# A decoder block's output projections behind attention: where inputs, results and gates are buffered, and when they are loaded

## The chip, the cores and the metric

The kernel runs on one core of a Trainium2 chip. The metric is the device time of one execution in microseconds; of several runs the median is given. A core has a matrix engine (PE, whose weight loads are a row of their own, PEld), a vector engine (DVE), a scalar engine (ACT), a general engine (POOL) and SyncE (SP), which here only issues transfers. Each engine takes its instructions in program order. "ACTq" and "SPq" mark what an engine's queue issues, transfers among it.

## The reference

One layer of a decoder block for 2048 tokens of width 1024, in float32. It has two branches, a gated linear recurrence and dilated windowed attention, each projected to 1024 columns; the two are merged with sigmoid gates and projected once more.

```
y_rnn  = (hr * silu(z_rnn)) @ w_out_rnn
y_attn = (o  * silu(z_attn)) @ w_out_attn
merged = sigmoid(g_r + bg_r) * y_rnn + sigmoid(g_a + bg_a) * y_attn
x      = x + gate * (merged @ w_o)
out    = rms_norm(x, g_final)
```

## The kernel before

**Precision.** Every float32 operand of a matmul is kept as two parts: a rounded high part, written by ACT (`hi_act`, L158), and the rest, a subtraction on POOL (`lo_pool`, L164) or DVE (`lo_dve`, L167). One product is three matmuls, high by high, high by low and low by high (`mm3`, all issued in L150).

**Work so far.** The input projections and the recurrence come first, then attention. Intermediate results lie in device memory, transposed: `oT` (attention, already times its gate), `yaT` (recurrence), `grT` and `gaT` (the merge gates), `mrT` (the recurrence's gated half of the merge), `meT` (the merged input of the last projection), `gateD` (the residual gate), and the output weights as they are in `wR` or split in `wD`.

**The two branch projections** are `steps` (L1658). There are eight jobs: the recurrence's output weights with four groups of 512 tokens, then attention's with the same four. A job has 8 tiles (one of 128 output columns each), a tile 8 steps over the inner dimension, a step 3 matmuls of 128x512. The 40 tiles t = 0 to 39 are laid between attention's operations. The last 24 (t = 40 to 63, from `TAIL0` = 40; jobs 5, 6 and 7, all of them attention's weights) come behind attention, and with them the loop `for s in range(LAST)` of 192 steps, s = 0 to 191. I count "steps of the tail" by this s. In these tiles a tile needs:

- *weights*, in two halves of four steps (`load_w`, L1675): raw from `wR` by SP into one of six buffers (S0 to S3, st3, st4), five halves ahead; `split_w` (k % 4 == 2) splits them two halves ahead, the low part on DVE for even halves and on POOL for odd ones;
- *inputs* y, eight slices of 128x512 for a job (`load_y`, `split_y`): load and split stand in the tables `LATE_LOAD_Y` and `LATE_SPLIT_Y`, by a step x that is 0 at the first step of the job's predecessor's last tile and 8 at the first step of the job itself. The split parts (`yh`, `yl`) have nine buffers each. The first five raw slices go to the four buffers R0 to R3 (`load_yd`, L346), the last three to the stages st1 and st2 (L1693);
- *gates*, two tiles `fg` from `gaT` and `mrT` out of four buffers (`load_g`, L1712), for tile t + 1 at k = 3 of tile t;
- *the eviction* of the tile before at k = 1 (`evict`): product times gate (L1718), plus the recurrence's half (L1720), both on DVE. The result goes to one of two buffers, s1 and s2 (the last two tiles: into the gate's buffer);
- *the store* of the tile before at k = 6 (`store`, L1726) to `meT`, by SP.

**Built beside the tail:** the right operands of the last projection. It uses a Strassen scheme (seven products instead of eight), so W_o, with its rows scaled by the residual gate, is turned into seven operands B11, T2, T3, T1, B21, T4, B22, each in a high and a low tile (`h`, `l`) of four 128x512 slices. `build_rows(x, k)` makes slice k of all of them from two rows of 128x1024 in st1 and st2: two gatings on POOL (L1859), combinations (L1867) and four low parts on DVE, three low parts on POOL, seven high parts on ACT. It starts at step x = 14, 75, 100 and 142 and is spread over 21 steps. The rows are loaded by `load_rows` (L1856) at x - 7 and x - 4, by SP for k = 0 and by ACT's queue otherwise. I call these builds 0 to 3.

**Behind the tail** comes the output stage, `output_pair`: eight pairs of 128 rows with seven products of 12 matmuls each, then the final norm.

What sets the order: everything here stands in `tc.manual_schedule()`, so that each engine takes its instructions as the code issues them. Waits for buffers follow from who used a buffer last. Transfers of SP and ACT share eight semaphores in turn: a transfer is issued only when the eighth before it has landed.

Of the kernel before, what the change touches and what calls it, by code (L numbers as in the profile page):

```python
# [10 lines left out]
F32 = mybir.dt.float32  # L11
# [9 lines left out]
P = 128  # L21
S = 2048
D = 1024
KT = D // P
NB = 4
CH = 512
H = 8
KH = KT // 2
# [61 lines left out]
def decoder_block(ctx, tc, x, c, positions, g_norm, w_mod, b_mod, w_in, b_gate, conv_w, conv_b,  # L90
# [4 lines left out]
    def T(pool, shape, dt, tag, **kw):  # L95
        cnt[0] += 1
        return pool.tile(shape, dt, tag=tag, name=f"{tag}_{cnt[0]}", **kw)
# [59 lines left out]
    def hi_act(o, i):  # L157
        nc.scalar.activation(o, i, AF.Copy)  # L158
# [175 lines left out]
    n_w, n_y, W, Y0 = [0], [0], {}, {}  # L334
# [151 lines left out]
    B = {}  # L486
# [10 lines left out]
    pR = pools.open("pR", side="right", bufs=1)  # L497
# [611 lines left out]
    for t in range(6):  # L1109
        pieces = []  # L1110
        i0 = t * P
        while i0 < (t + 1) * P:
            hd, i = divmod(i0, 96)
            n = min(96 - i, (t + 1) * P - i0)
# [154 lines left out]
    for f in range(2):  # L1269
# [20 lines left out]
        n = 0  # L1290
# [363 lines left out]
    TAIL0 = KT * (NB + 1)  # L1654
# [3 lines left out]
    def steps(jobs):  # L1658

        tiles = [(j, m) for j in range(len(jobs)) for m in range(KT)]  # L1660
        Y, G = {}, {}

        def load_w(x):

            if x < 2 * len(tiles):
                assert x == n_w[0]
                j, m = tiles[x // 2]
                if x <= RAW:
                    load_wd(jobs[j][0], m, x % 2)
                    return  # L1670

                n_w[0] += 1
                i = (x - 2 * TAIL0) % 6
                W[x] = t = T(pS, [P, 2, KH, P], F32R, f"S{i}") if i < 4 else T(fp, [P, 2, KH, P], F32R, f"st{i - 1}")
                nc.sync.dma_start(t[:, 1].bitcast(F32), wR[m, x % 2])  # L1675

        def split_w(x):
            if RAW < x < 2 * len(tiles):
                raw = W[x][:, 1].bitcast(F32)
                hi_act(W[x][:, 0], raw)  # L1680
                (lo_pool if x % 2 else lo_dve)(W[x][:, 1], raw, W[x][:, 0])

        def load_y(j, k, t):
            if j < len(jobs):
                w, ys, n = jobs[j]
                assert ys is yaT or (n // 2, k, n % 2) in stored
                if t >= TAIL0 and k > 4:
                    n_y[0] += 1
                    i, half = divmod(k - 5, 2)
                    if half == 0:  # L1690
                        v["y", j] = stage(1 + i, [P, D])
                    Y0[False, n, k] = y = v["y", j][:, half * CH : (half + 1) * CH]
                    nc.sync.dma_start(y, ys[k * P : (k + 1) * P, n * CH : (n + 1) * CH])  # L1693
                    return
                load_yd(ys, n, k)

        def split_y(j, k):
            if j < len(jobs):
                Y[j, k] = yh, yl = [T(fl, [P, CH], F32R, tag, bufs=NY) for tag in ("yh", "yl")]
                w, ys, n = jobs[j]  # L1700
                t = Y0.pop((ys is yaT, n, k))
                hi_act(yh[:], t[:])
                (lo_dve if k % 2 else lo_pool)(yl[:], t[:], yh[:])

        def load_g(t):
            j, m = tiles[t]
            w, ys, n = jobs[j]
            at_ = slice(m * P, (m + 1) * P), slice(n * CH, (n + 1) * CH)
            G[t] = []
            for src in (grT,) if ys is yaT else (gaT, mrT):  # L1710
                g = T(fl, [P, CH], F32, "fg", bufs=4)
                nc.sync.dma_start(g[:], src[at_])  # L1712
                G[t].append(g)

        def evict(t, ps):
            g = G[t]
            o = T(fp, [P, CH], F32, f"s{1 + t % 2}") if TAIL0 <= t < TAIL0 + 22 else g[0]
            nc.vector.tensor_tensor(o[:], ps[:], g[0][:], ALU.mult)  # L1718
            if len(g) > 1:
                nc.vector.tensor_tensor(o[:], o[:], g[1][:], ALU.add)  # L1720
            g[0] = o

        def store(t):
            j, m = tiles[t]
            w, ys, n = jobs[j]
            nc.sync.dma_start((mrT if ys is yaT else meT)[m * P : (m + 1) * P, n * CH : (n + 1) * CH], G.pop(t)[0][:])  # L1726

        for k in range(KT):
            split_y(0, k)
        yield  # L1730
        last = None
        for t, (j, m) in enumerate(tiles):
            ps = T(pj, [P, CH], F32, "pj")
            for k in range(KT):
                x = 2 * t + k // KH
                if k % KH == 1:

                    if x < 2 * TAIL0:
                        load_w(x + 3)
                    for x1 in range(x + 3 if x == 2 * TAIL0 else x + 5, x + 6) if x >= 2 * TAIL0 else ():  # L1740
                        load_w(x1)
                if k % KH == 2 and x >= 2 * TAIL0:
                    split_w(x + 2)
                if k == 1 and t:
                    evict(t - 1, last)
                if t < TAIL0:
                    if k == 3:
                        load_g(t)
                    if k == 7 and t:
                        store(t - 1)  # L1750
                else:
                    if k == 0 and t == TAIL0:
                        load_g(t)
                    if k == 3 and t + 1 < len(tiles):
                        load_g(t + 1)
                    if k == 6:
                        store(t - 1)
                wt = W[2 * t + k // KH]
                yh, yl = Y[j, k]
                mm3(ps[:], wt[:, 0, k % KH, :], wt[:, 1, k % KH, :], yh[:], yl[:], first=k == 0, last=k == KT - 1)  # L1760
                if k % KH == KH - 1:
                    W.pop(2 * t + k // KH)


                x = m * KT + k - KT * (KT - 1)
                j1 = j + 1
                if m == 0:
                    x, j1 = x + KT * KT, j

                for k1 in (LATE_LOAD_Y if t >= TAIL0 else LOAD_Y).get(x, ()) if j1 else ():  # L1770
                    load_y(j1, k1, t)
                for k1 in (LATE_SPLIT_Y if t >= TAIL0 else SPLIT_Y).get(x, ()) if j1 else ():
                    split_y(j1, k1)
                yield
            last = ps
        evict(len(tiles) - 1, last)
        store(len(tiles) - 1)

# [10 lines left out]

    LOAD_Y = {-12: [0], -10: [1], -8: [2], -6: [3], -2: [4], 4: [5], 5: [6], 6: [7]}  # L1790
    SPLIT_Y = {-3: [0], 3: [1], 4: [2], 5: [3], 7: [4], 10: [5], 11: [6], 12: [7]}
    LATE_LOAD_Y = {-12: [0], -10: [1], -8: [2], -6: [3], -2: [4], -1: [5, 6], 3: [7]}
    LATE_SPLIT_Y = {-3: [0], 1: [1], 2: [2], 3: [3], 6: [4], 8: [5], 9: [6], 11: [7]}
    fill = steps([(0, yaT, n) for n in range(NB)] + [(1, oT, n) for n in range(NB)])
    next(fill)
    with tc.manual_schedule():
# [37 lines left out]
    fp = pools.open("fp", bufs=1)  # L1834
# [4 lines left out]
    def stage(i, shape, dt=F32):  # L1839
        return T(fp, shape, dt, f"st{i}")  # L1840
# [3 lines left out]
    def on(n, fn, *args):  # L1844
        pend.setdefault(n, []).append((fn, args))
# [5 lines left out]
    v = {}  # L1851
# [206 lines left out]
    with tc.manual_schedule():  # L2058
        def load_gate():
            v["gate"] = stage(0, [P, D])  # L2060
            nc.sync.dma_start(v["gate"][:], gateD[0:1, :].broadcast_to([P, D]))

        on(5, load_gate)
        for k, x in enumerate((14, 75, 100, 142)):
            build_rows(x, k)
            for i in range(2):
                on(x - 7 + 3 * i, load_rows, k, i)
        on(LAST - 20, load_left, 0)
        for p in range(NP):
            for d, fn, args in left_events(p):  # L2070
                x = 7 * p + d - 4
                if p or d > 2:
                    on_p(max(x, 1), fn, *args)
                else:
                    on(LAST - 9 + 3 * (d + 1), fn, *args)
            if p:
                on_p(max(7 * p - 12, 0), load_left, p)
            if p > 1:
                on_p(7 * p - 2, load_rows_x, p)
        for s in range(LAST):  # L2080
            next(fill)
            fire(s)
        next(fill, None)
        fire(LAST)
        assert not pend
        pools.close("fl", "pR")
        up.append(pools.open("up", side="right", bufs=1))
        fire_p()
        load_rows_x(0)
        load_rows_x(1)  # L2090
        v["gf"] = T(up[0], [P, D], F32, "gf")
        nc.sync.dma_start(v["gf"][:], g_final.unsqueeze(0).broadcast_to([P, D]))
        for p in range(NP):
            output_pair(p)
        assert not after
# [30 lines left out]
```

## Time and profile before

| | |
|---|---|
| median of 3 runs | 2239.18 us (2237.68 to 2239.68) |
| the profiled execution's own time | 2237.5 us |
| its span, first to last instruction | 2235.7 us |
| granted matrix clock, mean | 0.993 |
| PE, DVE, ACT, POOL busy | 97%, 65%, 58%, 49% |
| bytes moved | 573.41 MB, mean 256 GB/s |

How to read it: the page's busy shares are means over stages with different limits. A waiting matmul is drawn as busy for part of its wait, so lost matrix time is found by counting matmuls in a stretch, not from the share. "L150" is the helper that issues all matmuls, so stages are told apart by the tile they write: `pj` is a tile of the branch projections, X, Z, W, V and Y are products of the Strassen schemes. A row such as `SPq L1712 <- DVE s L1718` says that SP's queue waited with the instruction of line 1712 for DVE's instruction of line 1718 that wrote (or read) tile s. Times in a view of a stretch count from the start of the span.

### The profile page before, as it was taken

Reading aid. Unit: us, or ns where it says so; the run is one execution under the profiler, and the core shown is the slowest. Engines: PE = TensorE matmul, PEld = TensorE weight load, DVE = VectorE, ACT = ScalarE, POOL = GpSimd, SP = SyncE. Lnnn points to the kernel's source line nnn. Section 1 sums busy time; section 2 is a strip of 40 time slices with the busy share of each in tenths; the row PEclk is TensorE's granted clock in tenths of the full one; section 3 lists DMA queues with packets and bytes.
Section 4 is the critical chain, followed back from the end, with each engine's and each line's share of the span. In section 5 each row is a group of like instructions: output and inputs, shape, how many; then the busy total and the mean of one; then the engine's idle time right before and its main releaser. Section 6 shows DMA issues by size and latency. Waiting matters only on the chain.

```text
span 2235.7 us, 34221 instructions
## 1 busy us (share of the span) xinstructions
PE 2173.8 (97%) x11326; PEld 1833.5 (82%) x11326; DVE 1448.3 (65%) x2475; ACT 1288.2 (58%) x2570; POOL 1093.0 (49%) x807
## 2 busy tenths in 40 slices
PE   8999999999999999999999999999999999989998
PEld 5998888888777998888888887888888988767886
DVE  5838887878455815544445342666777777669787
ACT  6637678668543627457547202777888886333333
POOL 2457777767556423222223112555666664556443
PEclk9999999999999999999999999999999999999999
DMA  8367887887998378888999988878887777888543
GB/s 286 116 212 256 289 292 270 291 283 269 321 282 288 112 225 270 288 286 283 306 303 298 360 293 275 261 228 266 265 272 228 238 250 228 259 278 275 182 162 111
DMA packets 412277, 573.41 MB, mean 256 GB/s; under 512 B 72422, under 2 KB 270274, under 8 KB 411076
## 3 DMA queue, kind: packets, MB, share of 16 engines
q1 hardware_dynamic: 369892, 442.82, 63.1%
q10 hardware_dynamic: 42016, 128.36, 15.1%
q8 instruction: 90, 1.47, 0.3%
q14 instruction: 87, 0.71, 0.1%
q0 software_dynamic: 192, 0.05, 0.0%
HBM read 352.99 MB, written 218.11 MB: 255 GB/s over the span
## 4 chain that ended last, share of the span: by engine, by line
PE 49%; DMA 8%; issue 4%; DVE 3%; POOL 3%; ACT 2%; SPq 2%; ACTq 0%; POOLq 0%; DVEq 0%
PE X L150 10%; PE V L150 9%; PE pj L150 7%; PE W L150 5%; PE Z L150 5%; PE Y L150 4%; PE sc L150 3%; PE o L150 3%; PE pg L150 1%; DMA R<-in_w_in_dram 1%; DMA meT<-s 1%; PE pT L1505 1%; DMA kraw<-qT 1%; PE pT L1518 1%; DMA S<-wD 1%
## 5 line engine op out<-in xcount | busy, mean ns | idle before, releaser
L150 PE MATMUL pj<-yh,S 128*128 128x512 f32 x896 | 331.5, 411 | 11.9 <-DVE S L167 5.2
L164 POOL TENSOR_TENSOR S<-R,S 128x512 fp32r<-128x512 f32 x168 | 256.8, 1536 | 170.1 <-ACT S L158 67.7
L150 PE MATMUL X<-T,S 128*128 128x512 f32 x1344 | 324.5, 390 | 5.4 <-POOL S L164 4.4
L150 PE MATMUL V<-T,S 128*128 128x512 f32 x1344 | 324.6, 390 | 4.0 <-DVE t L454 3.7
L150 PEld LDWEIGHTS X<-T,S 128*128 128x128 f32 x1344 | 251.4, 188 | 60.4 <-POOL S L164 5.3
L150 PEld LDWEIGHTS V<-T,S 128*128 128x128 f32 x1344 | 251.7, 188 | 58.7 <-ACT S L158 3.3
L150 PEld LDWEIGHTS pj<-yh,S 128*128 128x128 f32 x896 | 171.2, 192 | 47.9 <-DVE S L167 6.9
L164 POOL TENSOR_TENSOR S<-s,S 128x512 fp32r<-128x512 f32 x92 | 139.9, 1520 | 114.0 <-ACT S L158 73.2
L150 PE MATMUL pj<-yl,S 128*128 128x512 f32 x448 | 178.9, 399 | 2.9 <-DVE yl L167 1.5
L1421 ACT ACTIVATE pp<-pp,st 128x256 f32<-128x256 f32 (+3 forms) x256 | 133.5, 523 | 59.9 <-DVE st L1420 59.5
L150 PE MATMUL Z<-T,S 128*128 128x512 f32 x672 | 162.0, 390 | 0.0
L150 PE MATMUL Y<-T,S 128*128 128x512 f32 x672 | 161.8, 390 | 0.0
L150 PE MATMUL W<-T,S 128*128 128x512 f32 x672 | 161.7, 389 | 0.0
L150 PEld LDWEIGHTS W<-T,S 128*128 128x128 f32 x672 | 126.0, 188 | 27.0 <-issue 0.9
L167 DVE TENSOR_TENSOR ptl<-pT,pth 128x384 fp32r<-128x384 f32 (+1 forms) x160 | 97.8, 628 | 77.1 <-ACT pth L158 74.9
L150 PEld LDWEIGHTS Y<-T,S 128*128 128x128 f32 x672 | 125.9, 188 | 26.1
L150 PEld LDWEIGHTS Z<-T,S 128*128 128x128 f32 x672 | 125.8, 188 | 26.1
L164 POOL TENSOR_TENSOR s<-R,s 128x512 fp32r<-128x512 f32 x32 | 45.7, 1430 | 204.9 <-ACT s L158 170.9
L912 DVE SCALAR_TENSOR_TENSOR xc<-xr,par,xc 128x512 f32<-128x512 f32 x96 | 99.0, 1031 | 47.5 <-ACT xc L906 45.3
L158 ACT ACTIVATE S<-R 128x512 fp32r<-128x512 f32 x168 | 101.6, 622 | 48.3 <-DMA R<-in_w_in_dram 17.1
L1485 ACT ACTIVATE pp<-pp,M 128x256 f32<-128x256 f32 (+3 forms) x256 | 118.0, 523 | 9.6 <-DVE M L1608 9.6
L1420 DVE CUSTOM_DVE_ANT_0 pp<-sc,msk 128x256 f32<-128x256 f32 (+3 forms) x256 | 103.6, 447 | 28.0 <-PE sc L150 27.0
(405 smaller groups left out, 4993.1 us busy)
## 6 DMA issues: line engine op xcount, KB each, us to landing
sD<-S ACTq DMA_DIRECT2D x196, 512.0 KB, 4.2
S<-sD SPq DMA_DIRECT2D x196, 512.0 KB, 5.3
S<-wD SPq DMA_DIRECT2D x82, 512.0 KB, 5.5
R<-in_w_in_dram SPq DMA_DIRECT2D x136, 256.0 KB, 4.3
wD<-s ACTq DMA_DIRECT2D x64, 256.0 KB, 5.4
T<-in_w_mod_dram SPq DMA_DIRECT2D x8, 1024.0 KB, 11.7
vN<-ev SPq DMA_DIRECT2D x64, 128.0 KB, 2.7
zaT<-ev SPq DMA_DIRECT2D x32, 256.0 KB, 4.4
```

What stands on the lines that cost most here:

```text
L150: nc.tensor.matmul(o, lhsT=l, rhs=r, start=st, stop=sp, **kw)
L158: nc.scalar.activation(o, i, AF.Copy)
L164: nc.gpsimd.tensor_tensor(o, i, h.bitcast(F32), ALU.subtract)
L167: return nc.vector.tensor_tensor(o, i, h.bitcast(F32), ALU.subtract).ins
L912: nc.vector.scalar_tensor_tensor(xc, xr[:, i : i + CH], cw(i), xc, ALU.mult, ALU.add)
L1420: nc.vector.tensor_tensor_reduce(pdst, s_ps, mask, 1.0, 3e38, ALU.add, ALU.min, m_)
L1421: nc.scalar.activation(pdst, pdst, AF.Exp, bias=m_, scale=-1.0, accum_out=l_)
L1485: nc.scalar.activation(pp, pp, AF.Copy, scale=w)
L1505: nc.tensor.transpose(pt[:, c0 + j * P : c0 + (j + 1) * P], pp[i][:, k * P : (k + 1) * P], ident)
L1518: nc.tensor.transpose(pt[:, c * P : (c + 1) * P], pp[:, half * P : (half + 1) * P], ident)
```

## The change

Line numbers of the changed kernel are two lower from L1691 on.

- Inputs: from tile 40 on, all eight raw slices of a job land in the last slice (index 3) of T2, T3, T1 and T4, high and low tiles in turn; R0 to R3, st1 and st2 are no longer used for them. Job 5's inputs, loaded while t < 40, still go to R0 to R3.
- Their times: the late tables hold for jobs 6 and 7 only; the eight loads come at x = -20, -18, ... -6, and the splits of the last four slices one or two steps earlier than before. Job 5 keeps the ordinary tables, so that its last three splits come one or two steps later.
- Results: every tile from 40 on is evicted into R0 to R3 in turn.
- The store of tile t - 1 moves from k = 6 to k = 7, and the gates of tile t + 1 from k = 3 to k = 7, behind that store.
- Build 1 starts at step 72 instead of 75, and all W_o rows are loaded three steps earlier against their build (x - 10 and x - 7).

```diff
-                if t >= TAIL0 and k > 4:
+                if t >= TAIL0:
                     n_y[0] += 1
-                    i, half = divmod(k - 5, 2)
-                    if half == 0:
-                        v["y", j] = stage(1 + i, [P, D])
-                    Y0[False, n, k] = y = v["y", j][:, half * CH : (half + 1) * CH]
+                    name, l = (("T2", 0), ("T2", 1), ("T3", 0), ("T3", 1), ("T1", 0), ("T1", 1), ("T4", 0), ("T4", 1))[k]
+                    Y0[False, n, k] = y = B[name][l][:, KH - 1, :].bitcast(F32)
...
-            o = T(fp, [P, CH], F32, f"s{1 + t % 2}") if TAIL0 <= t < TAIL0 + 22 else g[0]
+            o = T(pR, [P, CH], F32, f"R{t % 4}") if t >= TAIL0 else g[0]
...
-                    if k == 3 and t + 1 < len(tiles):
-                        load_g(t + 1)
-                    if k == 6:
+                    if k == 7:
                         store(t - 1)
+                        if t + 1 < len(tiles):
+                            load_g(t + 1)
...
-                for k1 in (LATE_LOAD_Y if t >= TAIL0 else LOAD_Y).get(x, ()) if j1 else ():
+                for k1 in (LATE_LOAD_Y if j1 > NB + 1 else LOAD_Y).get(x, ()) if j1 else ():
                     load_y(j1, k1, t)
-                for k1 in (LATE_SPLIT_Y if t >= TAIL0 else SPLIT_Y).get(x, ()) if j1 else ():
+                for k1 in (LATE_SPLIT_Y if j1 > NB + 1 else SPLIT_Y).get(x, ()) if j1 else ():
                     split_y(j1, k1)
...
-    LATE_LOAD_Y = {-12: [0], -10: [1], -8: [2], -6: [3], -2: [4], -1: [5, 6], 3: [7]}
-    LATE_SPLIT_Y = {-3: [0], 1: [1], 2: [2], 3: [3], 6: [4], 8: [5], 9: [6], 11: [7]}
+    LATE_LOAD_Y = {2 * k - 20: [k] for k in range(KT)}
+    LATE_SPLIT_Y = {-3: [0], 1: [1], 2: [2], 3: [3], 5: [4], 6: [5], 8: [6], 9: [7]}
...
-        for k, x in enumerate((14, 75, 100, 142)):
+        for k, x in enumerate((14, 72, 100, 142)):
             build_rows(x, k)
             for i in range(2):
-                on(x - 7 + 3 * i, load_rows, k, i)
+                on(x - 10 + 3 * i, load_rows, k, i)
```

## The prediction

> **What bounds the kernel now.** The page first: its head and the busy row of the matrix engine.
>
> ```profile
> span 2235.7 us, 34221 instructions
> PE 2173.8 (97%) x11326; PEld 1833.5 (82%) x11326; DVE 1448.3 (65%) x2475; ACT 1288.2 (58%) x2570; POOL 1093.0 (49%) x807
> ```
>
> 97% says little, since a waiting matmul is drawn long. The rate tells more. The chain of waits, in order of time, has undisturbed runs of twelve 128x512 matmuls; one such row gives 2.72 / 12 = 0.2267 us each.
>
> ```profile
> 926.94 2.72 PE X L150 x12
> ```
>
> The change touches only what comes behind attention: 24 tiles (t = 40 to 63) of 8 steps of 3 matmuls, 576 x 0.2267 = 130.6 us of matmuls; a step is 0.68 us, a half 2.72, a tile 5.44. They run from about 1915 (tile 40) to 2073.75, where the first output product begins. The stretch view (PE alone: length, busy with its count, clock granted, DMA share, GB/s) splits that time at the stalls seen in the timeline.
>
> ```profile
> 1917.97:1925.68 7.71, 5.84 (x17) 0.78 0.77 251
> 1938.58:1946.18 7.60, 5.53 (x17) 0.78 0.98 339
> 1950.71:1953.14 2.43, 1.20 (x6) 1.00 0.58 122
> 1970.83:1976.96 6.13, 4.29 (x15) 1.00 0.93 290
> 1985.12:1990.22 5.10, 4.22 (x17) 1.00 0.84 273
> 1994.80:2010.70 15.90, 11.44 (x39) 0.89 0.81 250
> 2021.38:2035.42 14.04, 10.42 (x37) 0.88 0.76 240
> 2057.20:2059.01 1.81, 1.64 (x7) 1.00 0.77 213
> 1915.00:2074.00 159.00, 142.85 (x578) 0.96 0.83 268
> ```
>
> Length less count x 0.2267 (the count less the one or two matmuls that lie across the edges) is lost time: 4.3, 4.0, 1.5, 3.0, 1.5, 7.5, 5.9 and 0.5 us, which I call A to H: 28.2 us, and 159 - 130.6 = 28.4 agrees. Part of each loss is a slow clock after the wait (0.78 in A and B). Behind it the output stage runs without a gap, as this row shows (20 us hold 88 matmuls), so what the tail saves comes off the end one for one.
>
> ```profile
> 2094.00:2114.00 20.00, 20.00 (x90) 16.57 (x89) 16.23 (x28) 5.69 (x12) 9.05 (x6) 1.00 0.21 76
> ```
>
> Who ends those waits, from the timeline (start, length, idle before it and releaser): weights split late, or inputs split late.
>
> ```profile
> 1921.96 0.80 PE L150 MATMUL pj<-yl,S 128*128 128x512 f32 x1 [1.16 <-POOL yl L164]
> 1941.03 0.74 PE L150 MATMUL pj<-yh,S 128*128 128x512 f32 x2 [2.07 <-POOL S L164]
> 2006.25 0.84 PE L150 MATMUL pj<-yh,S 128*128 128x512 f32 x2 [1.61 <-DVE S L167]
> 2027.64 1.22 PE L150 MATMUL pj<-yh,S 128*128 128x512 f32 x2 [2.61 <-DVE S L167]
> ```
>
> Behind the splits stand the views of the waits, of SyncE's queue (the first row; total, times, longest) and of three engines. The gate loads of L1712 wait for the eviction that frees their buffers, and SyncE issues in order, so the weights behind them are late. The eviction waits for the store out of its buffer, of which there are two. POOL's gating of W_o rows waits for their load, and ScalarE waits for the gating with weight splits queued behind it.
>
> ```profile
> SPq L1712 <- DVE s L1718: 37.3, 17, 5.0
> DVE s L1718 <- DMA meT<-s: 12.6, 4, 5.9
> POOL st L1859 <- DMA st<-in_w_o_dram: 13.3, 5, 5.1
> ACT B11h L158 <- POOL st L1859: 14.2, 4, 7.1
> ACT S L158 <- DMA S<-wR: 12.8, 5, 4.4
> ACT S L158 <- POOL T1l L164: 2.5, 1, 2.5
> ```
>
> **The change part by part.** No instruction is added or removed; the built program has as many on every engine. Only places, buffers and order change.
>
> *Results in R0 to R3.* An eviction reuses a buffer after four tiles (21.8 us), no longer after two. The 12.6 us of waits on stores go. What is late next is the matmul it evicts or DVE's own backlog.
>
> *Gates at k = 7 behind the store.* SyncE's order per tile becomes weights, weights, store, gates. The weights for the second half no longer stand behind gates that wait for DVE. These rows of SyncE's queue show the price today: a weight load, then nothing until the gates are free 5.4 us later, then the next weights, which come out in F.
>
> ```profile
> 1988.68 0.32 SPq L1675 DMA_DIRECT2D S<-wR  x1
> 1994.10 0.32 SPq L1712 DMA_DIRECT2D fg<-gaT  x1
> 1995.79 0.37 SPq L1675 DMA_DIRECT2D st<-wR  x1
> ```
>
> The wait does not vanish: the store at k = 7 waits for the same DVE add, and behind it are two gate loads and the next tile's first weights. But it stands after this tile's second weight load, so DVE may lag 5.4 us behind the tile's start, against 2.7, before a weight load is held. The longest wait above is 5.0.
>
> *Inputs into T slices.* The eight loads of jobs 6 and 7 go out at steps 36 to 50 and 100 to 114 of the tail, eight steps ahead of their old start, into slices nobody needs before step 157: no wait for them in the built program. This removes D's late inputs. More important, stages st1 and st2 are no longer lent to inputs, so job 6 doesn't hold W_o rows back: rows for build 1 go out at steps 62 and 65, build at 72. POOL's 13.3 us and most of ScalarE's 14.2 us should go, and with them the start of E and F.
>
> *Split order for job 5.* Its last three inputs still load from L346 and land as before, and their splits now stand behind a weight split and the eviction of tile 39. I leave A at 4.3 (between 3.5, since the eviction no longer waits behind them, and 5.5, if the weight split ahead of them lands last). Weights 83 to 85 go out about 4 us earlier.
>
> What is not removed is the work on DVE and POOL. When both read SBUF they take turns. The third row is the next POOL operation: 1.68 us hold one POOL and one DVE operation, each drawn 1.7 long, while alone a DVE one is 0.68 long and starts 0.6 after its predecessor.
>
> ```profile
> 2025.31 1.72 POOL L164 TENSOR_TENSOR S<-S 128x512 fp32r<-128x512 f32 x1
> 2025.83 1.75 DVE L167 TENSOR_TENSOR S<-S 128x512 fp32r<-128x512 f32 x1
> 2026.99 1.72 POOL L164 TENSOR_TENSOR yl<-R,yh 128x512 fp32r<-128x512 f32 x1
> 2008.41 0.68 DVE L167 TENSOR_TENSOR B11l<-st,B11h 128x512 fp32r<-128x512 f32 x1
> L1859 POOL TENSOR_TENSOR st<-st,st 128x1024 f32<-128x1024 f32 x8 | 20.2, 2529 | 13.3 <-DMA st<-in_w_o_dram 13.3
> ```
>
> So a POOL split holds the pair about 1.1 us (1.68 - 0.6), a DVE one 0.6. A build of one row pair: 2 x 2.5 + 3 x 1.1 + 8 x 0.6 = 13.1; tiles need 1.1 + 2 x 0.6 = 2.3 each, 6.0 over the build's 21 steps. That is 19 us against 14.3 of matmuls. Two rows with all columns (DVE third, POOL fifth) test it: build 3, and build 2 from its second gating to job 7's last split.
>
> ```profile
> 2037.04:2059.39 22.35, 22.18 (x98) 18.07 (x97) 21.76 (x20) 8.07 (x14) 14.87 (x9) 1.00 0.84 259
> 2008.78:2034.58 25.80, 22.22 (x87) 17.21 (x85) 23.33 (x21) 11.83 (x21) 20.95 (x12) 0.91 0.86 280
> ```
>
> Build 3 took 22.35 us and the matmuls ran on (98 in the row): a lag of 5 to 8 us is covered by weights split ahead, and H costs 0.5. So builds 0 and 1, fed in time, should cost little as well: B 4.0 to 0.3, C 1.5 to 0.5, E 1.5 to 0.3. Build 2 is followed at once by job 7's eight splits (4 x 1.1 + 4 x 0.6 = 6.8 more), and its 25.8 us hold only 86 x 0.2267 = 19.5 of matmuls. Nothing of that work goes, so I leave G at 5.5 (bounds 3 and 7). Job 6's splits have no build beside them: D 3.0 to 0.8. In F, ScalarE's row loads for build 2 still wait for build 1's last POOL split (the 2.5 us row), with weight splits behind them: F 7.5 to 2.0, between 0 and the 4.9 that falls behind 2000.
>
> The Trainium skill has a rule on this (SBUF — State Buffer, "Who interferes with whom"): a DVE instruction with two SBUF inputs contends with a GpSimd one that reads SBUF, and the second fully blocks. The 1.68 us rows agree; were the two free to overlap, G would go too, which is the second case below.
>
> *Transfers.* The tail moves the same bytes in less time.
>
> ```profile
> DMA packets 22503, 42.55 MB, mean 268 GB/s; under 512 B 2422, under 2 KB 3446, under 8 KB 22492
> 1959.00:1972.00 13.00, 12.44 (x55) 1.00 1.01 343
> ```
>
> The second row is full: 343 GB/s at share 1.01. At 340, 42.55 MB need 125 us, so transfers allow 145 us of tail, but at 86%; a burst of eight inputs among tile traffic is again over the limit for some us. I charge 1 us for that, between 0 and 5. The Trainium skill names about 358 GB/s for HBM (the same page, "Summary: rules for kernel authors"), which as an estimate from that page would be 119 us; no stretch quoted here reaches it, and the row decides.
>
> **Sum.** After: A 4.3, B 0.3, C 0.5, D 0.8, E 0.3, F 2.0, G 5.5, H 0.5 = 14.2, and 1 for transfers: 15.2 of 28.2 remain, 13 saved. The profiled execution took 2237.5 us (span 2235.7 and 1.8 around it), so 2224.5; the median of the runs is 2239.18, 1.7 above it, so **2226**.
>
> **The rivals.**
>
> *More goes (0.14).* Early inputs and rows let DVE and POOL work ahead, and G melts as well: what remains is A, H and 1 for transfers, 22.4 saved, 2217. For: POOL is idle 13.3 us for rows now. Against: the 25.8 us row is nearly solid work.
>
> *The builds bind (0.17).* With feeding mended, the turn-taking and ScalarE's in-order row loads stop the matmuls where the queue did. Only B and D go, less 1: 6 saved, 2233. For: 19 us of work against 14.3 in each build. Against: build 3.
>
> *Slower (0.06): gates land too late.* They now leave after the store of t-1 and are needed by the eviction of t+1. Two tiles are 10.9 us; 0.3 until the eviction starts, 1.4 for its two operations and 1.2 for three issues leave 8.0 for landing. Beyond it, DVE waits in order with the splits behind it, and each us over costs half a us a tile. The landings now (kind, KB, median; then minimum, median, maximum of the gate tiles):
>
> ```profile
> fg<-gaT SPq DMA_DIRECT2D x24, 256.0 KB, 5.1
> DMA to landing us min/median/max: 3.2/5.2/7.6
> ```
>
> At 9.5 us throughout, 24 x 0.75 = 18 us more on top of 2226: 2244. Against: today's worst is 7.6, at 0.83 mean share.
>
> *It doesn't do what it says (0.05).* If DVE lags over 5.4 us in most tiles, the store holds weights as the gates did, and the gain is lost: 2239.
>
> **How the numbers follow.** Forecast 0.58 (2220 to 2231 by the bounds of A, F, G and transfers). The range 2216 to 2236 holds nearly all of it, half of the first rival and nearly all of the second: about 0.8. A measurement here tells about 0.2%, 4.5 us, from no change; the second rival reaches 2235 and beyond with a quarter of its chance. Faster: 0.58 + 0.14 + 0.13 = 0.85. Same: 0.05 + 0.04 = 0.09. Slower: 0.06.
>
> **What would show it.** Right: SyncE's waits for evictions under 15 us, now at the store; no wait of DVE on stores to meT; POOL's wait for W_o rows under 5; matmul gaps left only near tile 40 (some 4 us) and around job 7's first tile (some 5); weight loads at their half's start. Wrong: DVE waiting on fg loads (gates late); gaps in builds 0 and 1 with weights landed in time (the pair binds); no gap around job 7 (G mis-sized); a gap in the output stage, which I hold untouched.

## The result and the profile after

| | before | after |
|---|---|---|
| median, runs of one session | 2239.18 us (2237.68 to 2242.84) | 2232.37 us (2227.96 to 2234.33) |
| the profiled execution | 2237.5 us | 2230.96 us |
| its span | 2235.7 us | 2229.2 us |
| tail: first matmul of tile 40 to first output product | 1914.80 to 2073.75, 158.9 us | 1914.56 to 2067.19, 152.6 us |

The ratio of the times is 0.9965 (95% interval 0.9953 to 0.9976): 6.8 us or 0.35% faster; 13 had been forecast. The tail got 6.3 us shorter, and nothing ahead of it or behind it moved by more than 0.3 us. The head of the changed kernel's page shows next to nothing of it:

```profile
span 2229.2 us, 34199 instructions
PE 2170.3 (97%) x11326; PEld 1835.1 (82%) x11326; DVE 1454.1 (65%) x2475; ACT 1287.5 (58%) x2570; POOL 1095.9 (49%) x807
```

So again PE alone by stretches (from, to, length, busy with its count, granted clock, DMA share, GB/s), cut at the stalls A, C, D, F and G, and last the whole tail:

```profile
1917.73:1925.80 8.07, 5.98 (x17) 0.79 1.04 390
1946.49:1947.90 1.41, 0.82 (x4) 1.00 0.88 328
1969.14:1970.00 0.86, 0.55 (x3) 1.00 1.01 379
1988.34:1999.20 10.86, 7.14 (x29) 1.00 0.91 295
2009.72:2031.10 21.38, 14.43 (x46) 0.84 0.67 207
1915.00:2067.30 152.30, 138.64 (x576) 0.97 0.85 279
```

Length less 0.2267 us for each matmul but the one on the edge gives 4.4, 0.7, 0.4, 4.5 and 11.2 us. B, E and H have no stall left. From the first matmul of tile 40 to the first output product it is 152.6 - 576 x 0.2267 = 22 us lost, where 28.4 were. But half of what is left now stands in one place, G, and G has doubled. The timeline of PE (start, length, idle before it and releaser) says what ended the waits in F and G:

```profile
1990.70 0.50 PE L150 MATMUL pj<-yh,S 128*128 128x512 f32 x1 [1.98 <-ACT S L158]
1992.07 0.73 PE L150 MATMUL pj<-yh,S 128*128 128x512 f32 x2 [0.64 <-POOL S L164]
1998.93 0.73 PE L150 MATMUL pj<-yh,S 128*128 128x512 f32 x2 [1.11 <-POOL S L164]
2012.74 0.73 PE L150 MATMUL pj<-yh,S 128*128 128x512 f32 x2 [2.63 <-POOL S L164]
2018.38 0.73 PE L150 MATMUL pj<-yh,S 128*128 128x512 f32 x2 [1.03 <-DVE S L167]
2025.15 0.50 PE L150 MATMUL pj<-yl,S 128*128 128x512 f32 x1 [1.72 <-DVE yl L167]
2027.93 1.22 PE L150 MATMUL pj<-yh,st 128*128 128x512 f32 x2 [1.58 <-DVE st L167]
```

All of G's four waits are for a low part, of a weight or of an input, from DVE or POOL; together 6.96 us of idle PE. Most of the other 4.3 us of G are matmuls at the slow clock that follows (0.84 in the row of that stretch).

The waits that the change was to remove are gone or moved, by the view of the waits (total, times, longest):

```profile
SPq L1675 <- PE pj L150: 42.2, 28, 4.0
SPq L1724 <- DVE R L1718: 21.6, 11, 5.0
DVE R L1716 <- DMA fg<-gaT: 2.3, 1, 2.3
POOL st L1857 <- DMA st<-in_w_o_dram: 2.8, 1, 2.8
ACT S L158 <- POOL T1l L164: 1.8, 1, 1.8
```

SyncE now waits mostly for the matmuls to release weight buffers (42.2): it runs as far ahead as the buffers let it. DVE no longer waits for a store to meT (12.6 before), and POOL waits 2.8 us for W_o rows (13.3 before). DVE waits once for a gate, 2.3 us, and ScalarE 1.8 us for build 1's last POOL split (2.5 before). What grew is not a wait of these queues. DVE and POOL over the same chain of work, from build 2's first gating to the last input split of job 7 (length, PE, PEld, DVE, ACT, POOL), the kernel before and then the changed one:

```profile
2003.28:2034.58 31.30, 25.88 (x96) 19.50 (x94) 28.21 (x26) 14.60 (x26) 25.01 (x14) 0.89 0.87 275
```

```profile
1994.81:2025.10 30.29, 23.85 (x94) 17.83 (x92) 30.12 (x24) 13.90 (x25) 27.87 (x16) 0.94 0.84 275
```

The matmuls ahead of it lost less, but this chain is as long as before (30.3 against 31.3 us), and DVE was busy for 30.12 of 30.29 us. The matmuls arrive earlier and wait there; how much of G that accounts for, e3 below shows.

### The profile page after: what moved, and what is told of

Same layout as the page of the kernel before. It is cut to its first block, busy times and chain, and to the rows that moved or that the text cites. A ratio compares the mean times of both kernels' runs of the same rounds, so it can differ in the third digit from the quotient of the medians.

```text
span 2229.2 us, 34199 instructions
## 1 busy us (share of the span) xinstructions
PE 2170.3 (97%) x11326; PEld 1835.1 (82%) x11326; DVE 1454.1 (65%) x2475; ACT 1287.5 (58%) x2570; POOL 1095.9 (49%) x807
## 4 chain that ended last, share of the span: by engine, by line
PE 53%; DMA 5%; DVE 4%; issue 3%; ACT 2%; POOL 2%; SPq 1%; ACTq 0%; POOLq 0%; DVEq 0%
PE X L150 10%; PE V L150 10%; PE pj L150 9%; PE W L150 5%; PE Z L150 5%; PE Y L150 4%; PE sc L150 3%; PE o L150 3%; PE pg L150 1%; PE pT L1505 1%; PE pT L1518 1%; ACT pp L1421 1%; DMA R<-yaT 1%; POOL q L1382 1%; DMA S<-wD 1%
## 6 DMA issues: line engine op xcount, KB each, us to landing
T<-in_w_mod_dram SPq DMA_DIRECT2D x8, 1024.0 KB, 11.7
```

## The experiments

After seeing this I had two theories. **T1, feeding:** build 2 starts late, because its rows wait in ScalarE's queue behind build 1 and then land in 8.0 us (median of ScalarE's six, 6.3 before) among job 7's early inputs. **T2, the pair:** DVE and POOL take turns, and build 2 with job 7's splits needs them for 30 us, whatever the feeding. The table holds all runs. Loss is counted as above, from the starts of the matmuls in the timeline, summed over these steps of the tail: A 0 to 20, B to 36, C to 50, D to 80, E to 94, F to 116, G to 145, H to the end.

| kernel | A | B | C | D | E | F | G | H | sum | median us | ratio to before, 95% |
|---|---|---|---|---|---|---|---|---|---|---|---|
| before | 4.5 | 4.0 | 1.5 | 3.0 | 1.5 | 7.5 | 5.9 | 0.5 | 28.4 | 2239.18 | |
| after | 4.5 | 0.0 | 0.9 | 0.6 | 0.0 | 4.6 | 11.3 | 0.1 | 22.1 | 2232.37 | 0.9953 to 0.9976 |
| e5_after_again | 4.4 | 0.0 | 0.9 | 0.6 | 0.0 | 3.9 | 11.6 | 0.1 | 21.4 | 2229.97 | 0.9954 to 0.9982 |
| e1_two_buffers | 4.2 | 0.0 | 1.0 | 0.3 | 0.0 | 4.9 | 7.8 | 0.2 | 18.4 | 2231.02 | 0.9969 to 0.9993 |
| e2_gates_k3 | 2.5 | 2.0 | 3.1 | 0.3 | 0.0 | 6.6 | 5.5 | 0.1 | 20.2 | 2230.54 | 0.9959 to 0.9985 |
| e3_inputs_late | 4.1 | 0.0 | 1.0 | 0.4 | 0.0 | 4.7 | 6.8 | 0.1 | 17.2 | 2226.97 | 0.9936 to 0.9970 |
| e4_rows_early | 3.9 | 0.0 | 1.1 | 0.2 | 0.0 | 1.4 | 10.8 | 0.1 | 17.5 | 2230.97 | 0.9956 to 0.9982 |
| e6_rows_early_gating_dve | 4.3 | 0.0 | 1.1 | 0.7 | 0.0 | 1.9 | 7.7 | 0.1 | 15.7 | 2222.24 | 0.9920 to 0.9963 |
| e7_builds_early | 2.5 | 0.0 | 1.8 | 1.6 | 2.9 | 1.1 | 5.6 | 1.5 | 17.2 | 2226.91 | 0.9948 to 0.9972 |
| e8_build2_behind | 4.3 | 0.0 | 0.9 | 3.0 | 0.0 | 1.0 | 8.2 | 4.0 | 21.3 | 2234.49 | 0.9977 to 1.0003 |
| e9_tail_on_dve | 3.7 | 0.0 | 0.0 | 0.0 | 0.0 | 0.0 | 1.6 | 0.0 | 5.3 | 2213.02 | 0.9873 to 0.9908 |
| e10_window_on_dve | 4.3 | 0.0 | 1.0 | 0.5 | 0.0 | 0.2 | 1.7 | 0.0 | 7.6 | 2218.10 | 0.9907 to 0.9937 |
| e11_after_on_dve | 2.0 | 0.0 | 0.1 | 0.0 | 0.0 | 0.9 | 2.1 | 0.0 | 5.1 | 2214.41 | 0.9881 to 0.9927 |
| e12_before_on_dve | 3.8 | 7.1 | 0.0 | 1.9 | 0.5 | 2.2 | 6.0 | 0.0 | 21.5 | 2227.55 | 0.9951 to 0.9972 |

Medians and losses don't follow each other to the microsecond: in these profiles the tail begins anywhere from 1910.0 to 1920.5 us, with nearly the same instructions ahead of it (in e9, e11 and e12 the even input splits of job 5 that fall there are on DVE too). So a difference of 2 or 3 us in the medians says nothing here. The sums of one profile each are better, and the two profiles of the changed kernel (after, e5) agree within 0.7 us in every column; what e1, e2 and e3 show below in G is a larger step.

### Build 2's first row early: e4_rows_early

```diff
     def load_rows(k, i):
-        v[k, i] = t = stage(1 + i, [P, D])
+        if (k, i) == (2, 0):
+            v[k, i] = [T(fp, [P, CH], F32, f"s{1 + j}") for j in range(2)]
+            for j in range(2):
+                nc.scalar.dma_start(v[k, i][j][:], w_o[0, k * P : (k + 1) * P, j * CH : (j + 1) * CH])
+            return
+        v[k, i] = t = stage(1 if k == 2 else 1 + i, [P, D])
...
-                on(x - 10 + 3 * i, load_rows, k, i)
+                on(x - (22 if (k, i) == (2, 0) else 10 - 3 * i), load_rows, k, i)
```

> The changed kernel, but build 2's first row is loaded 12 steps earlier into buffers that lie idle there (s1 and s2, so its gating becomes two instructions), and its second row goes to st1, which build 1 leaves before st2. Theory T1 (the builds are fed too late: the row loads stand in ScalarE's queue behind build 1, then land 8 us later among job 7's input loads): POOL no longer waits 2.8 us for a row, the gap at job 7 falls from 11.3 to about the 5.5 us forecast and the one before it from 4.5 to about 2, in all 2224 to 2227 us. Theory T2 (the pair: build 2 and job 7's splits take DVE and POOL, which take turns, for 30 us where the matmuls of those steps take 24): the work only starts earlier and the gap at job 7 stays at 9 us or more, in all 2230 to 2232 us.

F fell from 4.6 to 1.4, G stayed at 10.8. POOL gates the first row without waiting, and waits 1.35 us for the second:

```profile
1994.18 2.99 POOL L1864 TENSOR_TENSOR s<-s,st 128x512 f32<-128x512 f32 x2
1999.77 2.67 POOL L1866 TENSOR_TENSOR st<-st,st 128x1024 f32<-128x1024 f32 x1 [1.35 <-DMA st<-in_w_o_dram]
```

So T1 is right for F and wrong for G. The median (2230.97) is in T2's range.

### Job 7's inputs late again: e3_inputs_late

```diff
-                for k1 in (LATE_LOAD_Y if j1 > NB + 1 else LOAD_Y).get(x, ()) if j1 else ():
+                for k1 in (LAST_LOAD_Y if j1 > NB + 2 else LATE_LOAD_Y if j1 > NB + 1 else LOAD_Y).get(x, ()) if j1 else ():
...
+    LAST_LOAD_Y = {-12: [0], -10: [1], -8: [2], -6: [3], -2: [4], -1: [5, 6], 3: [7]}
```

> The changed kernel, but the raw inputs of job 7 are loaded by the table of before (steps -12 to 3 instead of -20 to -6), still into the slices of the operands. T1: build 2's rows meet fewer transfers and land in about 6 us instead of 8, so the gap at job 7 falls by 2 to 4 us, 2228 to 2230 us. T2: the pair's work is the same, the gap stays, 2232 us. If the early loads are what feeds the first splits of job 7, it rises instead by 1 to 4 us, 2233 to 2236 us.

F is unchanged (4.7), so the early inputs don't make build 2 late, as T1 had it. G fell to 6.8, against T2's "the gap stays", and the median, 2227.0 us, is below all three ranges. Rows that came sooner explain little of it: build 2's first gating starts 78.7 us after the tail does, against 80.3 in the changed kernel, but of these 1.5 us only 0.7 are left at DVE's last input split but one, and up to step 128 the matmuls lose as much. DVE's last input split and the weight split behind it (start, length), the changed kernel first:

```profile
2023.35 1.75 DVE L167 TENSOR_TENSOR yl<-T4l,yh 128x512 fp32r<-128x512 f32 x1
2025.02 2.85 DVE L167 TENSOR_TENSOR st<-st 128x512 fp32r<-128x512 f32 x1
```

```profile
2021.93 0.68 DVE L167 TENSOR_TENSOR yl<-T4l,yh 128x512 fp32r<-128x512 f32 x1
2022.54 0.68 DVE L167 TENSOR_TENSOR st<-st 128x512 fp32r<-128x512 f32 x1
```

In the changed kernel the first runs beside a weight split of POOL, and the second, on which the matmul at 2027.93 waits, beside POOL's two gatings of build 3 (the row below); in e3 these begin at 2024.33, behind it.

```profile
2024.51 5.59 POOL L1857 TENSOR_TENSOR st<-st,st 128x1024 f32<-128x1024 f32 x2
```

In the kernel before, POOL gates for build 3 from 2037.04 on, 2.5 us behind job 7's last split. The rows that the change loads three steps earlier against their build brought these gatings forward into G, by the issues of their loads: 2015.42 and 2016.71 in the changed kernel, 2031.02 and 2034.60 before. No run put the old loading steps back alone, so this isn't tested.

What the meeting costs, e3 shows. Behind step 136, where the matmul of 2027.93 stands, the matmuls lose 3.3 us in the changed kernel (3.5 in e5), and nothing in e3 or in the kernel before. B to F lose as much in e3 as in the changed kernel (6.1 us each), so the matmuls arrive as early; G is 6.8 all the same, 0.9 above before. The other runs agree: the weight split behind the last input split takes 2.85 us in the changed kernel, e4, e5, e6 and e8, and behind step 136 they lose 1.9 to 4.3 us; it takes 0.68 in e2, e3 and e7, and they lose nothing there. (In the kernel before it stands ahead of the last input split.) So of the 5.4 us by which the change made G longer, e3 leaves about 1 to the earlier matmuls and some 4 to what the last splits run beside. Which operations meet turns on a microsecond; why the late inputs shift it I can't tell.

### The parts of the change undone: e1_two_buffers, e2_gates_k3

```diff
-            o = T(pR, [P, CH], F32, f"R{t % 4}") if t >= TAIL0 else g[0]
+            o = T(fp, [P, CH], F32, f"s{1 + t % 2}") if TAIL0 <= t < TAIL0 + 22 else g[0]
```

> The changed kernel, but results go to the two buffers of before (s1, s2) instead of R0 to R3; the rest of the change is kept. My prediction put the end of DVE's 12.6 us of waits for stores down to the four buffers and gave them parts of the gaps B to D: by it DVE waits for stores 8 us or more again and the time is 2234 to 2238 us. The rival is that loading the gates behind the store and the inputs early are enough: waits for stores under 3 us, 2232 us.

The rival holds, nearly to its number. B to E are as in the changed kernel; with two buffers DVE waits for a store once:

```profile
DVE s L1716 <- DMA meT<-s: 3.3, 1, 3.3
```

The median, 2231.0, agrees. G is 7.8 here; the two DVE operations shown for e3 take 0.68 and 1.78 us, since the gatings of build 3 begin at 2021.20, when the second (from 2020.01) is mostly done.

```diff
-                    if k == 7:
-                        store(t - 1)
-                        if t + 1 < len(tiles):
-                            load_g(t + 1)
+                    if k == 3 and t + 1 < len(tiles):
+                        load_g(t + 1)
+                    if k == 6:
+                        store(t - 1)
```

> The changed kernel, but the gates of the next tile are loaded at k = 3 again and the store stands at k = 6, as before. By my prediction the weights then stand behind gates that wait for the eviction, SyncE's wait for evictions goes from 21.6 back to some 35 us, and B, D, E and part of F return: 2236 to 2240 us. If four result buffers and early inputs carry the gain alone: 2231 to 2233 us.

The losses came back in part where expected, B 2.0, C 3.1 and F 6.6 (D and E did not), and SyncE's queue waits for evictions ahead of the gates again:

```profile
SPq L1710 <- DVE R L1716: 33.1, 14, 6.6
```

But G fell to 5.5, and the sum, 20.2, is no larger than the changed kernel's; the median, 2230.5, is below both ranges. That looks like a trade of B, C and F for G, but build 3's gatings stand behind the chain's last splits here as in e3:

```profile
2034.15 5.65 POOL L1857 TENSOR_TENSOR st<-st,st 128x1024 f32<-128x1024 f32 x2
```

The last input split and the weight split behind it take 0.68 us each, from 2031.76 and 2032.36 on. Against e3, which doesn't have that meeting either, the gates at k = 3 lose 3.0 us more in the tail.

### The changed kernel again: e5_after_again

> The changed kernel once more, unaltered, to see how far one profile of the tail can be trusted: both theories expect the same gaps, A 4.5, F 4.5 and G 11.3 us, within about 1.5 us in each, and 2229 to 2233 us.

As expected: F 3.9, G 11.6 and a median of 2230.0 us.

### Less work on POOL beside job 7: e6, e7 and e8

e6 is e4_rows_early with one more edit, in both branches of `gate_rows`:

```diff
-        nc.gpsimd.tensor_tensor(v[k, i][:], v[k, i][:], v["gate"][:], ALU.mult)
+        (nc.vector if k == 2 else nc.gpsimd).tensor_tensor(v[k, i][:], v[k, i][:], v["gate"][:], ALU.mult)
```

> Build 2's rows early as before in e4_rows_early, and the two gatings of build 2 on DVE instead of POOL. T2 (the pair DVE/POOL is what is short): a gating holds the pair 2.8 us on POOL and less on DVE alone, so the gap at job 7 shrinks by about as much as the two save, 2 to 4 us against e4_rows_early, 2227 to 2229 us. T1 (only the feeding): with the rows in time already nothing is left to gain, the gap stays as in e4_rows_early.

G fell by 3.1 against e4, as T2 has it. The median is some 5 us below its range; the profile has 1.8 us less loss than e4's, so most of that doesn't come from the tail.

```diff
-        for k, x in enumerate((14, 72, 100, 142)):
+        for k, x in enumerate((14, 66, 94, 142)):
```

> The changed kernel with builds 1 and 2 six steps earlier (66 and 94 instead of 72 and 100): build 2 then ends at step 115, before job 7's splits begin at 117. The rows are loaded as late before their build as in the changed kernel. T2: build and splits no longer need the pair at once, the gap at job 7 falls from 11 to 2 to 5 us, 2223 to 2227 us. T1: the rows still wait behind build 1 and still land late, so that the start of build 2 and the gaps F and G move, but stay as long: 2230 to 2233 us.

G is 5.6 and F 1.1, but D and E lose 4.5 instead of 0.6: build 1 now follows at once on job 6's splits. Time within T2's range; the gap not quite.

```diff
-        for k, x in enumerate((14, 72, 100, 142)):
+        for k, x in enumerate((14, 72, 130, 153)):
...
-            (nc.sync if p else nc.scalar).dma_start(t[:], meT[half * KH * P : (half + 1) * KH * P, p * 2 * P : (p + 1) * 2 * P]
+            nc.sync.dma_start(t[:], meT[half * KH * P : (half + 1) * KH * P, p * 2 * P : (p + 1) * 2 * P]
```

> The changed kernel with build 2 at step 130, behind job 7's splits, and build 3 at 153, whose first row is loaded early into s1 and s2 (its second into st1; the left operands of the last projection are loaded by SyncE instead of ScalarE's queue). T2: F and G go almost entirely (2 us or less each), because nothing but the tiles' splits is left on the pair while job 7's inputs are split; the two builds next to each other may give back 1 to 4 us later; 2222 to 2227 us. If job 7's splits alone make the gap, whatever is built beside them, G stays at 6 us or more, 2228 to 2233 us.

T2's expectation failed for G, which is 8.2 with build 2 behind it by the steps, and the median, 2234.5, is above both ranges. But this run doesn't isolate job 7's splits, as three rows show:

```profile
2006.54 0.63 ACT L158 ACTIVATE yh<-T2l 128x512 fp32r<-128x512 f32 x1 [5.29 <-PE pj L150]
2019.28 2.82 POOL L1866 TENSOR_TENSOR st<-st,st 128x1024 f32<-128x1024 f32 x1
2019.80 2.85 DVE L167 TENSOR_TENSOR st<-st 128x512 fp32r<-128x512 f32 x1
```

ScalarE waits 5.29 us until the matmuls release a yh buffer. There are nine, so the split of slice 1 can't begin before job 6's last tile has used its own slice 0, at step 120, and the other seven must be done within 15 steps, 10.2 us, however early the inputs land. And POOL gates for build 2 before they are done, ahead of the steps at which I had placed it: G has build 2's gatings in it, beside a weight split of 2.85 us as in the changed kernel. That job 7's splits alone make a gap is not shown. The total is worse for another reason: SyncE, in order, issued the left operands at 2060.61 instead of 2048.44 and 2052.93, and the output stage began with a gap:

```profile
2070.93 0.73 PE L150 MATMUL X<-B11h,st 128*128 128x512 f32 x2 [3.50 <-DVE st L167]
```

### POOL's work on DVE: e9, e10, e11 and e12

```diff
-                (lo_pool if x % 2 else lo_dve)(W[x][:, 1], raw, W[x][:, 0])
+                (lo_pool if x % 2 and not x >= 2 * TAIL0 else lo_dve)(W[x][:, 1], raw, W[x][:, 0])
...
-                (lo_dve if k % 2 else lo_pool)(yl[:], t[:], yh[:])
+                (lo_dve if k % 2 or j > NB else lo_pool)(yl[:], t[:], yh[:])
...
-        nc.gpsimd.tensor_tensor(v[k, i][:], v[k, i][:], v["gate"][:], ALU.mult)
+        (nc.vector if k >= 0 else nc.gpsimd).tensor_tensor(v[k, i][:], v[k, i][:], v["gate"][:], ALU.mult)
...
-        lo(B[name][1][:, k, :], part(name, k), B[name][0][:, k, :])
+        (lo_dve if k >= 0 else lo)(B[name][1][:, k, :], part(name, k), B[name][0][:, k, :])
```

This stands on e4_rows_early in e9, on the changed kernel in e11 and on the kernel before in e12. In e10, also on e4_rows_early, the conditions are `25 <= x - 2 * TAIL0 <= 35`, `j > NB + 2` and `k >= 2`.

> As e4_rows_early (first row of build 2 early), and from tile 40 to the output stage POOL does nothing: its weight splits, input splits, low parts of the builds and gatings are all on DVE. If the loss comes from DVE and POOL taking turns (theory T2: a split takes 1.7 us on each while both run, 0.6 to 0.7 us on DVE alone, so two splits cost 1.3 us on DVE and 1.7 us on the pair), the gap at job 7 falls below 4 us and the time to 2219 to 2224 us. If the amount of element-wise work is the limit, or DVE's strict order (a low part, a gating or an eviction that waits now holds up all the others), G stays at 7 us or more or gaps open elsewhere: 2227 to 2236 us.

> As e9_tail_on_dve, but only for what falls to steps 100 to 140 and for build 3: the weight splits of these steps, job 7's input splits, builds 2 and 3. T2: F and G as in e9_tail_on_dve (G under 4 us) and nothing else changes, 2219 to 2224 us. With the amount or DVE's order as the limit: G 7 us or more, 2227 to 2232 us.

T2 holds, and by more than I had expected: 2213.0 us in e9, 1.1% below before, with G 1.6 (ratio 0.9891, interval in the table), and 2218.1 in e10, with F 0.2 and G 1.7. The tail of e9 in one row (length, PE, PEld, DVE, ACT, POOL):

```profile
1917.00:2052.20 135.20, 132.69 (x575) 108.49 (x574) 109.72 (x170) 53.92 (x94) 0.00 (x0) 0.99 0.92 312
```

In the changed kernel the row is 152.30 us long, with DVE busy 123.80 and POOL 91.89 us:

```profile
1915.00:2067.30 152.30, 138.64 (x576) 110.00 (x575) 123.80 (x117) 53.42 (x94) 91.89 (x52) 0.97 0.85 279
```

DVE does 170 operations in 109.72 us instead of 117 in 123.80: it took over all of POOL's work and was busy for less time. The groups of instructions show how (count, busy us, mean ns), the changed kernel first, then e9:

```profile
L1718 DVE TENSOR_TENSOR R<-R,fg 128x512 f32<-128x512 f32 x23 | 24.4, 1061 | 1.5 <-DMA fg<-mrT 0.8
L167 DVE TENSOR_TENSOR S<-S 128x512 fp32r<-128x512 f32 x15 | 18.6, 1238 | 3.8 <-ACT S L158 3.8
L1716 DVE TENSOR_TENSOR R<-pj,fg 128x512 f32<-128x512 f32 x23 | 15.7, 685 | 18.1 <-PE pj L150 15.8 <-DMA fg<-gaT 2.3
L1857 POOL TENSOR_TENSOR st<-st,st 128x1024 f32<-128x1024 f32 x8 | 21.3, 2670 | 4.8 <-DMA st<-in_w_o_dram 2.8 <-DMA meT<-R 1.1 <-DMA st<-gateD 0.9
```

```profile
L167 DVE TENSOR_TENSOR S<-S 128x512 fp32r<-128x512 f32 x30 | 20.2, 686 | 5.2 <-ACT S L158 5.1
L1716 DVE TENSOR_TENSOR R<-pj,fg 128x512 f32<-128x512 f32 x24 | 16.5, 688 | 14.2 <-PE pj L150 14.2
L1718 DVE TENSOR_TENSOR R<-R,fg 128x512 f32<-128x512 f32 x23 | 15.9, 693 | 2.7 <-DMA fg<-mrT 2.0
L1866 DVE TENSOR_TENSOR st<-st,st 128x1024 f32<-128x1024 f32 x7 | 8.5, 1220 | 0.7 <-DMA st<-gateD 0.7
```

On average a weight split takes 1238 ns on DVE while POOL works in the tail and 686 without, the addition of L1718 1061 and 693. The product of L1716, whose one input comes from the matmuls' own memory, takes 685 and 688: it isn't touched. The Trainium skill has this split (SBUF — State Buffer, "Who interferes with whom"): a DVE instruction with at most one input in SBUF doesn't contend with GpSimd, one with two does. The three rows agree.

> The changed kernel with POOL's work of the tail on DVE, as in e9_tail_on_dve, but with build 2's rows loaded where the changed kernel loads them. If the early row does nothing once the pair is gone: 2212 to 2215 us as e9_tail_on_dve. If DVE, which now gates itself, is held up by the late row (2.8 us of waiting in the changed kernel, now with all splits queued behind it): 2 to 5 us more, 2215 to 2219 us.

2214.4 us, in the first range; the loss is 5.1 us, e9's 5.3. With the pair gone, the early row isn't needed.

> The kernel before with POOL's work of the tail on DVE: the old places, buffers and gate loads. If the engines' taking turns was the root of most of the 28 us lost there, 2212 to 2218 us, and the change is worth little beside it. If SyncE's waits for evictions and DVE's for stores are causes of their own, the gaps B, C, D and part of F stay, some 8 to 12 us: 2220 to 2228 us, and the change is worth as much on DVE as it was forecast to be worth, 8 to 13 us.

2227.6 us, in the second range; 21.5 us of loss remain. The queue's old waits are all there, and DVE, which now gates, waits up to 7.4 us for rows, with ScalarE and the matmuls behind it (the gap B). Waits of e12:

```profile
SPq L1712 <- DVE s L1718: 33.2, 17, 6.0
DVE st L1859 <- DMA st<-in_w_o_dram: 13.1, 3, 7.4
```

Between e12 and e11 lies the change alone, without POOL: 2227.55 to 2214.41, 13.1 us. The intervals of the two ratios put it at 0.24 to 0.91%, 5 to 20 us. With POOL it was worth 6.8, by its interval 5 to 11, so the medians alone don't show that it is worth more without; in the profiles the loss of the tail falls by 16.4 us (21.5 to 5.1), against 6.3.

## Why the prediction was right, and where it was not

**Sign, size and range.** Faster, as forecast, and within the range. The gain was half the 13 us: 22.1 us of loss remain against 15.2 forecast. Undoing one part at a time (e1, e2, e3) gave medians of 2227.0 to 2231.0 us, none above the changed kernel's 2232.4, so which part the gain in time belongs to is not shown; what follows goes by the losses in one profile each.

Three readings of the prediction don't hold. Its upper end of the forecast, 2231, is added up too low: its bounds for A, F, G and transfers make 1.2 + 2.9 + 1.5 + 4 = 9.6 us on top of 2226. "Part of each loss is a slow clock" holds for A, B, F and G alone; its rows for C, D, E and H show 1.00. And 343 GB/s was no limit: the changed kernel's stretch at A moved 390. The 1 us charged for transfers can't be told apart from the other losses.

**B, C, D, E, H: right.** 2.4 us were forecast for the five, 1.6 is left. For B and C it was SyncE's order in good part: with the gates at k = 3 and the store at k = 6 again (e2) they come back to 5.1 together, of 5.5 before. For D and E no run put the late inputs of job 6 or the shared stages back alone; their cause is argued from the waits. The four result buffers did nothing that shows: I had put the end of DVE's 12.6 us of waits down to them, but with two buffers and the other edits 3.3 us of waits remain and no loss comes back (e1).

**A: right.** 4.3 forecast, 4.5 measured; 4.4 again in e5.

**The wait at the store: wrong as a mark, right in effect.** "SyncE's waits for evictions under 15 us" failed: 21.6, the longest 5.0. It did no harm that shows: each was below the 5.4 us that the prediction worked out as the slack.

**Gates: right.** The landings are as they were, the longest of them under the 8.0 us that the prediction worked out (minimum, median, maximum). The sign named for late gates did come once: DVE waited 2.3 us for one, before the eviction at 2057.03, where the matmuls lose nothing (H is 0.1).

```profile
DMA to landing us min/median/max: 3.6/5.2/7.7
```

**F: the mechanism right, the size off.** "F 7.5 to 2.0" became 4.6. ScalarE's in-order row loads were named as its cause. What I didn't count is that the row then lands 8.0 us later, with POOL idle for 2.8 us; with the row early (e4) F is 1.4.

**G: the step that failed.** "Nothing of that work goes, so I leave G at 5.5 (bounds 3 and 7)." It is 11.3, 5.4 above before, and two things were missing. The larger, some 4 us by e3, is a meeting: build 3's gatings, which POOL now began at 2024.51, ran beside the last weight split of the chain (2.85 us instead of 0.68), and the last input split ran beside a weight split of POOL (1.75 instead of 0.68). I had counted the earlier row loads as moved at no cost; that they brought the gatings forward is read from their issues and not tested alone.

The smaller, about 1 us by e3, is this: I took the loss of a stretch as a property of its work. It is the work's length less the matmuls that stand beside it, and less the lead with which it starts. The chain of DVE and POOL took 30.3 us, as good as before, and ended 9.5 us sooner (2025.10 against 2034.58), while the matmuls, freed of 11.4 us in B to F (17.5 to 6.1), stood 11.7 us earlier in front of it (G's stretch begins at 2009.72, against 2021.38). So stalls removed ahead of a saturated pair come back at the pair, but here only a small part of the 11.4 us did.

The prediction did have the pair: 1.68 us for a split on each, 19 us of work for 14.3 of matmuls in a build, and "The builds bind" as a rival. The rival was wrong about the place. Builds 0 and 1, fed in time, cost next to nothing (B 0.0, D and E 0.6); it is build 2 with job 7's splits, and build 3's gatings behind them.

**T1 and T2.** T1 stands for F and falls for G (e4, e3). T2 stands for G, on e6, e9 and e10, with one correction from e3: G is not a fixed 30 us of work, but turns on what POOL does beside the chain's last splits. Job 7's splits are pressed into 15 steps by the nine yh buffers (e8); I read that off ScalarE's wait and didn't try more buffers.

## What to carry to other kernels

Before you price a repair of the feeding, look for the next chain of work that has no slack, and take from the gain what that chain will hand back: its length doesn't shrink because the matmuls arrive sooner (about 1 us here). Two engines that take turns on their operands are not two engines: price a split between them against the faster one alone, by its own undisturbed rows. And an early load lets an engine run ahead of its step: ask which work its instruction will then stand beside (some 4 us here).

## What the hardware showed beyond that

Taking an engine away was worth as much as the change: on the kernel before, POOL silent in the tail gave a ratio of 0.9962 (e12), the change 0.9965, and both together 0.9904 (e11, 2214.4 us). The undisturbed durations fit that. POOL needs 1.29 us for a split when DVE doesn't run beside it, DVE 0.68 (two rows of the changed kernel):

```profile
1955.08 1.29 POOL L164 TENSOR_TENSOR S<-S 128x512 fp32r<-128x512 f32 x1 [3.13 <-ACT S L158]
1954.12 0.68 DVE L167 TENSOR_TENSOR S<-S 128x512 fp32r<-128x512 f32 x1
```

Two splits cost about 1.3 us on DVE alone and 1.7 us on the two engines together. The Trainium skill says to put element-wise work on VectorE, with GPSIMD some two times slower (GPSIMD Engine Reference, "Engine selection"); 1.29 against 0.68 agrees. That sharing such work between the two can be slower than DVE alone is what these runs add. One split of each took 1.68 us together in the prediction's rows, less than the 1.29 + 0.60 of one after the other, so "the second fully blocks" holds only roughly here.
